# Seven products in place of eight for one more pair of k-tiles, and 1-f from a second sigmoid, in a bidirectional recurrence layer

## The chip, the cores and the metric

The kernel runs on one core of a Trainium2 chip. The metric is the time of one execution on the device in microseconds, the median of several runs.

## What is computed

One encoder layer over 256 tokens of width 2048, in fp32. Cut to what matters here:

```python
hn = _rmsnorm(h, norm_w[i])
proj = hn @ w_in[i]                                  # 2048 x 18432
q, v, f_fwd, f_bwd, z_a, b_gate, c_gate, h_b, z_b = jnp.split(proj, IN_SPLITS, axis=-1)
# each direction, 16 heads of 128, chunks of 64 tokens, q = silu(q):
f = lb + (1.0 - lb) * jax.nn.sigmoid(f_logit)
log_f = jnp.log(f)
k = 1.0 - f
b = jnp.cumsum(log_f, axis=-2)
q_rel = q * jnp.exp(b - b_mid)
k_rel = k * jnp.exp(b_mid - b)
scores = jnp.einsum('bhntk,bhnsk->bhnts', q_rel, k_rel)   # masked, times v; plus the carried state
# then: o_a normed per head, * silu(z_a); the short convolution's branch; w_out; gate; final norm
```

The weights of one layer are read once, some 260 MB with what the kernel writes and reads again.

## The kernel before

TensorE does the fp32 products as three products of rounded halves: each fp32 number is split into a high part (ScalarE, the cast of L121) and a low part, the rest (VectorE, the subtraction of L122), for the weights as they stream in as for the activations. Weights come by DMA on SP's queue into three raw buffers of 1 MB (`Stream.load`, L100), and `Stream.get` opens the parts three ahead of use, into five buffers of split parts (`spl`). `three` (L545 to L549) is one product of 128 rows, 128 tokens and 512 columns: three matmuls.

The projections of q, the two forget gates, v and z_a run for eight groups of two heads, called pairs 0 to 7 here, taken two at a time (`two_pairs`, i = 0, 2, 4, 6). For each of two pairs TensorE does the forward gate, the backward gate and q (`gemm_in`, L425 and L427, then `evac`, L487 on ScalarE and L488 on VectorE); then v and z_a of both pairs together (`gemm_vz`). v and z_a are summed over sixteen k-tiles of 128, in eight pairs of k-tiles q = 0 to 7 (`VZ_ORDER`, in the code called q as well). A pair of k-tiles is a 2 by 2 product of blocks (two halves of tokens, two k-tiles, and the two column blocks v and z_a). In plain form that is eight products of `three`, 24 matmuls. For the q in `VZ_SUMS` it is done with seven (`half`, the part behind `which.index(q)`), 21 matmuls, by sums of blocks of weights and of activations in Strassen's manner. Four banks of PSUM collect what goes into both outputs and are added at the end (L469 to L477).

The sums of activations, for each q of `VZ_SUMS`, are made once, in the projection stage of pair 2, and kept (`xsum`). The sums of weights are made in one of two ways. For the q in `VZ_OWN`, VectorE makes them in the raw buffer (`add_up`, L83, three additions of 128x1024). For other q in `VZ_SUMS`, DMAs make them in DRAM: `prepare` copies four blocks from the weights into a buffer in DRAM (SP's queue), `add_up` in the kernel's body adds to them in three steps of accumulating DMAs issued by GpSimd (L338, L342), and the stream then loads three blocks and the 1 MB of sums. Before the change all q of `VZ_SUMS` are in `VZ_OWN`, so no such sum is made for v and z_a; the output projection, later, makes sixteen (`sums`).

For each pair, `mix_forgets` (L605 to L629) scales by the norms on GpSimd (L492), takes the sigmoid of both gates' logits (L614, ScalarE), then for each direction and head the logarithm (L623, ScalarE) into `lf`, and 1-f on VectorE from the sigmoid, with `noml` = -(1-lb) and `oml` = 1-lb (L627). `mix_pair` (L667 on) makes the running sums (L678, L684), the differences to the middle of each chunk (L691, L694: `dd`), the factors across chunks (`ge`, from three small sums L700 to L702 and an exponential L703), and per direction exp(dd) into `pf` (L705), exp(-dd) into `dd` (L706), 1-f times `dd` (L707) and q times `pf` (L708). GpSimd makes from them `kc` and `qc` (L716, two of each, one for each direction) and `kx` (L722). `products` then does small matmuls of 128x32 on TensorE, sixteen kinds for each head and half (L735); their first reads `qc` of direction 1 and `dd`. Behind them are `cx` (L779, `kx` times `qc`), a masked copy on VectorE (L783) and a sum on GpSimd (L784: `s`).

What sets the order: TensorE's program is in the order of the code. A clock of ticks, one to three for a k-tile or pair of k-tiles of a projection, calls what `at(dt, fn)` has set. So the products of the first of two pairs stand early in the v/z_a stage, and those of the second pair (pair 3, 5, 7) run 32 ticks behind the end of it, in the first projection stage of what comes next (behind pair 7 that is the first projection of the convolution, whose `cg` is scaled on GpSimd at L492). On ScalarE, VectorE and GpSimd a scheduler sets the order of the instructions from priorities (`high_priority`: the splits and the evacuations stand ahead) and from when it reckons their inputs to be ready.

## Time and profile before

| | |
|---|---|
| median of 3 runs | 1111.57 us (1110.87 to 1111.96) |
| profiled execution, its time | 1112.2 us |
| profiled execution, its span | 1110.5 us |
| granted clock of TensorE | 0.998 |
| first product of pairs 3, 5, 7 (from the span's start) | 262.94, 380.37, 497.80 us |

The span is the time from the first to the last instruction that the profiler recorded. PE is TensorE and PEld its loading of weights, DVE is VectorE, ACT ScalarE, POOL GpSimd, SP the engine whose queue issues the loads. A row of the timeline gives the start, the duration, the engine, the line, the operation, and in square brackets how long the engine was idle ahead of it and what it waited for. Matmuls overlap: the distance of two starts is what one costs, not the duration in the row. A row of a group gives the busy time of all its instructions, the mean of one in ns, and the idle time ahead of them. [...]

### The profile page before, as it was taken

The page shows a single profiled execution, that of the slowest core. Times are in us where ns is not written, and L with a number is a line of the kernel's source. Part 1 is how long each engine was busy: PE and PEld are TensorE (multiplying, and loading weights), DVE is VectorE, ACT ScalarE, POOL GpSimd, SP SyncE. Part 2 cuts the span into 40 slices and gives each one's busy share as a digit, 9 for nine tenths or more (in the row PEclk, how much of TensorE's full clock was granted, in tenths as well). Part 3 has the DMA queues.
Part 4 walks back from the last instruction along what each step waited for, and adds up shares of the span by engine and source line. Part 5 has one row for each costly group of instructions (what it writes and reads, how often), then busy time and mean ns, then how long its engine had stood idle before and what let it go on. Part 6 is the DMA issues. An engine that isn't in the chain of part 4 may idle for free.

```text
span 1110.5 us, 16882 instructions
## 1 busy us (share of the span) xinstructions
PE 1100.5 (99%) x6455; PEld 945.7 (85%) x6455; DVE 851.4 (77%) x1127; ACT 677.3 (61%) x946; POOL 269.1 (24%) x215
## 2 busy tenths in 40 slices
PE   9999999999999999999999999999999999999997
PEld 8888888888888888888888888888888888888886
DVE  7799578896889778997657758856667888887673
ACT  6786577667876697575545535535546575575562
POOL 1045015203530325043334223424331000000101
PEclk9999999999999999999999999999999999999999
DMA  9755454564457744758999998999979887887542
GB/s 340 272 187 190 153 190 157 171 242 153 161 162 258 292 152 152 231 172 228 298 310 250 270 334 231 282 345 254 288 196 306 318 299 286 286 312 253 193 133 76
DMA packets 69808, 260.44 MB, mean 235 GB/s; under 512 B 7008, under 2 KB 16608, under 8 KB 52192
## 3 DMA queue, kind: packets, MB, share of 16 engines
q1 hardware_dynamic: 60480, 242.25, 62.1%
q0 software_dynamic: 8960, 16.78, 10.0%
q8 instruction: 51, 0.84, 0.3%
q10 hardware_dynamic: 288, 0.34, 0.1%
q14 instruction: 29, 0.24, 0.1%
HBM read 257.25 MB, written 35.65 MB: 264 GB/s over the span
## 4 chain that ended last, share of the span: by engine, by line
PE 98%; DMA 1%; ACT 0%; SPq 0%; DVE 0%; DVEq 0%; issue 0%; ACTq 0%
PE a L427 37%; PE a L425 19%; PE avz L547 3%; PE avz L548 3%; PE avz L549 3%; PE pg L1027 3%; PE pg L1026 3%; PE pg L1028 3%; PE pa L547 2%; PE pa L548 2%; PE pa L549 2%; PE a L446 1%; PE a L448 1%; PE a L447 1%; PE pb_sc L548 1%; PE pb_sc L549 1%
## 5 line engine op out<-in xcount | busy, mean ns | idle before, releaser
L122 DVE TENSOR_TENSOR spl<-raw,spl 128x1024 fp32r<-128x1024 f32 (+2 forms) x419 | 505.0, 1219 | 163.6 <-ACT spl L121 160.2
L427 PE MATMUL a<-xs,spl 128*128 128x512 f32 x1792 | 617.3, 395 | 0.6 <-ACT spl L121 0.6
L121 ACT CAST spl<-raw 128x1024 fp32r<-128x1024 f32 (+2 forms) x419 | 414.1, 999 | 255.0 <-PE a L425 81.9
L425 PE MATMUL a<-xs,spl 128*128 128x256 f32 x1792 | 483.8, 278 | 0.0
L427 PEld LDWEIGHTS a<-xs,spl 128*128 128x128 f32 x1792 | 332.2, 188 | 73.6 <-ACT spl L121 1.0
L425 PEld LDWEIGHTS a<-xs,spl 128*128 128x128 f32 x1792 | 334.6, 188 | 5.8 <-DVE spl L122 0.5
L1143 POOL TENSOR_TENSOR hh<-hh,fw 128x512 f32<-128x512 f32 (+1 forms) x9 | 11.0, 1227 | 250.7 <-ACT gt L1142 248.0
L487 ACT COPY r<-a 128x256 f32<-128x256 f32 x112 | 40.5, 368 | 37.3 <-PE a L425 35.8
L547 PE MATMUL avz<-spl,xs 128*128 128x512 f32 x138 | 54.0, 391 | 0.0
L549 PE MATMUL avz<-spl,xs 128*128 128x512 f32 x138 | 53.7, 389 | 0.0
L548 PE MATMUL avz<-spl,xs 128*128 128x512 f32 x138 | 53.7, 389 | 0.0
L1026 PE MATMUL pg<-spl,ht 128*128 128x512 f32 (+1 forms) x120 | 45.2, 377 | 0.0
L1027 PE MATMUL pg<-spl,ht 128*128 128x512 f32 (+1 forms) x120 | 45.1, 376 | 0.0
L1028 PE MATMUL pg<-spl,ht 128*128 128x512 f32 (+1 forms) x120 | 45.0, 375 | 0.0
L716 POOL TENSOR_TENSOR qc<-pf,ge 128x256 f32<-128x256 f32 x16 | 18.3, 1148 | 105.8 <-ACT dd L706 91.8
L492 POOL TENSOR_TENSOR xf<-xf,rbc 128x1024 f32<-128x1024 f32 x8 | 19.9, 2486 | 94.0 <-DVE rbc L403 50.2
L121 ACT CAST spl<-early 128x1024 fp32r<-128x1024 f32 (+1 forms) x29 | 28.7, 990 | 19.1 <-PE pb_y L549 7.5
L122 DVE TENSOR_TENSOR spl<-early,spl 128x1024 fp32r<-128x1024 f32 (+1 forms) x29 | 32.9, 1147 | 9.2 <-ACT spl L121 8.8
L547 PE MATMUL pa<-spl,mixa 128*128 128x512 f32 x88 | 34.5, 392 | 0.0
L549 PE MATMUL pa<-spl,mixa 128*128 128x512 f32 x88 | 34.3, 389 | 0.0
L548 PE MATMUL pa<-spl,mixa 128*128 128x512 f32 x88 | 34.2, 389 | 0.0
L716 POOL TENSOR_TENSOR kc<-dd,ge 128x256 f32<-128x256 f32 x16 | 27.7, 1728 | 19.8 <-DVE dd L707 13.6
(321 smaller groups left out, 1641.7 us busy)
## 6 DMA issues: line engine op xcount, KB each, us to landing
raw<-in_w_in_dram SPq DMA_DIRECT2D x106, 1024.0 KB, 6.9
raw<-in_w_in_dram SPq DMA_DIRECT2D x100, 256.0 KB, 3.9
raw<-in_w_out_dram SPq DMA_DIRECT2D x36, 512.0 KB, 5.2
sums<-in_w_out_dram SPq DMA_DIRECT2D x32, 512.0 KB, 10.6
raw<-in_w_in_dram SPq DMA_DIRECT2D x26, 512.0 KB, 5.2
raw<-sums SPq DMA_DIRECT2D x13, 1024.0 KB, 5.3
raw<-in_w_gate_dram SPq DMA_DIRECT2D x9, 1024.0 KB, 5.1
sums<-in_w_out_dram POOLq DMA_DIRECT2D x16, 512.0 KB, 10.1
```

The costliest lines, as they stand in the source:

```text
L121: self.nc.scalar.copy(out=v[:, :, 0], in_=r)
L122: self.nc.vector.tensor_tensor(out=v[:, :, 1], in0=r, in1=v[:, :, 0], op=ALU.subtract)
L425: pe.matmul(a[:, :T], lhsT=lhsT, rhs=xs[:, kt, 0, :], start=False, stop=(kt == NKT - 1))
L427: pe.matmul(a, lhsT=lhsT, rhs=xs[:, kt, :, :].rearrange("p s n -> p (s n)"), start=(kt == 0), stop=False)
L487: act.copy(out=r, in_=acc[m][:, 1, :])
L547: pe.matmul(acc, lhsT=ah, rhs=w[:, 0], start=start, stop=False)
L548: pe.matmul(acc, lhsT=ah, rhs=w[:, 1], start=False, stop=False)
L549: pe.matmul(acc, lhsT=al, rhs=w[:, 0], start=False, stop=stop)
L716: pool.tensor_tensor(out=c64(dst[:, d]), in0=c64(src[:, d, :, half * P : (half + 1) * P]), in1=g.unsqueeze(3).broadcast_to([P, 2, 2, CH]), ...
L1026: pe.matmul(acc[m], lhsT=lh, rhs=wh, start=(kt == 0), stop=False)
L1027: pe.matmul(acc[m], lhsT=lh, rhs=wl, start=False, stop=False)
L1028: pe.matmul(acc[m], lhsT=ll, rhs=wh, start=False, stop=(kt == nk - 1))
```

## The change

It has two parts that the diff shows, and the order that comes of them.

The first part puts q = 5 into `VZ_SUMS` but not into `VZ_OWN`. In each of the three v/z_a stages that use `half` (i = 2, 4, 6) that pair of k-tiles is done with seven products, and its sums of weights are made in DRAM by `prepare` and `add_up`, called at ticks 50, and 166, 196 and 220 (98, 104 and 110 for the first two pairs). `xsum` has four sets in place of three.

The second part makes 1-f as (1-lb) times the sigmoid of the negated logit. The first sigmoid goes to `lf`, and the logarithm is taken there in place; a second sigmoid with scale -1 takes the place of the logits in `xf`. The 32 instructions of L627 and `noml` go. Where L707 multiplied `xf` and `dd` for both heads in one instruction, `scalar_tensor_tensor` now does it for each head, with `oml` as its scalar (L705 in the kernel after). To make room for the larger `xsum`, some constants move to other buffers.

```diff
-    VZ_ORDER, VZ_SUMS, VZ_OWN = range(8), (2, 4, 6), (2, 4, 6)
+    VZ_ORDER, VZ_SUMS, VZ_OWN = range(8), (2, 4, 5, 6), (2, 4, 6)
...
-    wz = const.tile([P, P], F32, name="wz")
+    early = const.tile([P, 2048], F32, name="early")
+    wz = early[:, 1024 : 1024 + P]
...
-    mx = const.tile([P, 2, 16], F32, name="mx")
-    et = const.tile([P, 2, 2, 16], F32, name="et")
-    esum = const.tile([P, 2, 16], F32, name="esum")
+    mx = xp.tile([P, 2, 16], F32, name="mx")
+    et = xp.tile([P, 2, 2, 16], F32, name="et")
+    esum = xp.tile([P, 2, 16], F32, name="esum")
...
-    noml = const.tile([P, 2, 16], F32, name="noml")
...
-        dve.tensor_scalar(noml, oml, -1.0, None, op0=ALU.mult)
...
-    rw = [const.tile([P, P], F32, name=f"rw{m}") for m in range(2)]
...
+        rw.append(ap_.tile([P, 2, P], F32, tag="s", name="rw"))
...
-        act.activation(xf, xf, AF.Sigmoid)
+        lf = ap_.tile([P, 2, 2, T], F32, tag="lf", name=f"lf{i}")
+        act.activation(lf, xf, AF.Sigmoid)
         sg = ap_.tile([P, 2, T], F32, tag="sg", name=f"sq{i}")
         act.activation(sg, qt, AF.Sigmoid)
+        act.activation(xf, xf, AF.Sigmoid, scale=-1.0)
         pool.tensor_tensor(out=qt, in0=qt, in1=sg, op=ALU.mult)
 
-        lf = ap_.tile([P, 2, 2, T], F32, tag="lf", name=f"lf{i}")
         for d in range(2):
             for h in range(2):
                 hd = 2 * i + h
                 act.activation(
-                    lf[:, d, h, :], xf[:, d, h, :], AF.Ln,
+                    lf[:, d, h, :], lf[:, d, h, :], AF.Ln,
                     bias=lb[:, d, hd : hd + 1], scale=oml[:, d, hd : hd + 1],
                 )
-                dve.tensor_scalar(
-                    xf[:, d, h, :], xf[:, d, h, :], noml[:, d, hd : hd + 1], oml[:, d, hd : hd + 1],
-                    op0=ALU.mult, op1=ALU.add,
-                )
...
             act.activation(pv[d], dv[d], AF.Exp)
             act.activation(dv[d], dv[d], AF.Exp, scale=-1.0)
-            dve.tensor_tensor(out=dv[d], in0=xf[:, d], in1=dv[d], op=ALU.mult)
+            for h in range(2):
+                dve.scalar_tensor_tensor(
+                    out=dv[d][:, h], in0=xf[:, d, h], scalar=oml[:, d, 2 * i + h : 2 * i + h + 1], in1=dv[d][:, h],
+                    op0=ALU.mult, op1=ALU.mult,
+                )
             dve.tensor_tensor(out=pv[d], in0=qt, in1=pv[d], op=ALU.mult)
```

With fewer instructions on VectorE and more on ScalarE, the scheduler sets a different order on three engines. TensorE keeps its own, apart from the products of q = 5. The place shown is the first projection stage behind the v/z_a stage of pairs 2 and 3, in which pair 3's `mix_pair` runs. Here is GpSimd there, before (L716 makes `qc` and `kc`, L722 `kx`, L784 `s`):

```order
48 L784 TENSOR_TENSOR s_2059<-early 128x256 x2
49 L716 TENSOR_TENSOR qc_2400<-pf_2376,ge_2386 128x256
50 L716 TENSOR_TENSOR kc_2399<-dd_2377,ge_2386 128x256
51 L716 TENSOR_TENSOR qc_2400<-pf_2376,ge_2386 128x256
52 L716 TENSOR_TENSOR kc_2399<-dd_2377,ge_2386 128x256
53 L722 TENSOR_TENSOR kx_2405<-kc_2399,ge_2386 128x512
54 L784 TENSOR_TENSOR s_2617<-early 128x256
```

and after (the lines are one further on; `vz_5` is the buffer in DRAM for the sums of q = 5):

```order
48 L785 TENSOR_TENSOR s_2071<-early 128x256 x2
49 L717 TENSOR_TENSOR qc_2419<-pf_2393,ge_2403 128x256
50 L717 TENSOR_TENSOR kc_2418<-dd_2394,ge_2403 128x256 x2
51 L723 TENSOR_TENSOR kx_2424<-kc_2418,ge_2403 128x512
52 L717 TENSOR_TENSOR qc_2419<-pf_2393,ge_2403 128x256
53 L336 DMA vz_5_82<-in_w_in_dram 256x1x256 x2
54 L785 TENSOR_TENSOR s_2638<-early 128x256
```

The second `qc`, that of direction 1, has moved from between the two `kc` to behind `kx`, and the issue of the accumulating DMAs follows it.

ScalarE at the same place, before (L121 is the cast of a split, L487 half of an evacuation, L703 makes `ge`, L705 and L706 the exponentials, L802 the squares of an output):

```order
221 L703 ACTIVATE ge_2386<-gx 128x20
222 L706 ACTIVATE dd_2377<-dd_2377 128x512
223 L705 ACTIVATE pf_2376<-dd_2377 128x512
224 L802 ACTIVATE jk_2457,ss_1332<-o_2448 128x128
225 L487 COPY r<-a_4_0_2355 128x256
226 L121 CAST spl_2513<-raw_2511 128x4x256
227 L487 COPY r<-a_4_1_2356 128x256
228 L706 ACTIVATE dd_2377<-dd_2377 128x512
229 L802 ACTIVATE jk_2457,ss_1332<-o_2448 128x128 x3
230 L121 CAST spl_2532<-raw_2511 128x4x256
```

and after (`ge` is L700 there, the exponentials L702 and L703):

```order
224 L702 ACTIVATE pf_2393<-dd_2394 128x512
225 L121 CAST spl_2534<-raw_2532 128x4x256
226 L487 COPY r<-a_4_0_2372 128x256
227 L487 COPY r<-a_4_1_2373 128x256
228 L121 CAST spl_2553<-raw_2532 128x4x256
229 L700 ACTIVATE ge_2403<-gx 128x20
230 L703 ACTIVATE dd_2394<-dd_2394 128x512
231 L702 ACTIVATE pf_2393<-dd_2394 128x512
232 L703 ACTIVATE dd_2394<-dd_2394 128x512
233 L121 CAST spl_2574<-raw_2572 128x4x256
234 L121 CAST spl_2653<-raw_2572 128x4x256
```

`ge` and two exponentials have moved from ahead of the cast of the first of these parts, and one from between the two casts, to behind the second cast.

VectorE after the change, in the same stretch (L122 is the subtraction of a split, L488 the other half of an evacuation, L705 the new product, L709 the product with q, L784 the masked copy that waits for the products):

```order
255 L709 TENSOR_TENSOR pf_2393<-qt_1684,pf_2393 128x512
256 L122 TENSOR_TENSOR spl_2534<-raw_2532,spl_2534 128x4x256
257 L488 TENSOR_TENSOR xf_2370<-a_4_0_2372,r 128x256
258 L122 TENSOR_TENSOR spl_2553<-raw_2532,spl_2553 128x4x256
259 L488 TENSOR_TENSOR xf_2370<-a_4_1_2373,r 128x256
260 L705 SCALAR_TENSOR_TENSOR dd_2394<-xf_1683,oml,dd_2394 128x256 x3
261 L122 TENSOR_TENSOR spl_2574<-raw_2572,spl_2574 128x4x256
262 L705 SCALAR_TENSOR_TENSOR dd_2394<-xf_1683,oml,dd_2394 128x256
263 L709 TENSOR_TENSOR pf_2393<-qt_1684,pf_2393 128x512
264 L122 TENSOR_TENSOR spl_2653<-raw_2572,spl_2653 128x4x256
265 L488 TENSOR_TENSOR xf_2370<-a_4_0_2511,r 128x256
```

Three of the four products of 1-f stand behind the split of the second part (`spl_2553`), the fourth and the product with q behind that of the third.

More of the change, by code (lines that the diff above doesn't have):

```diff
@@ L273, in tile_hymba_encoder @@
     pool.memset(ones, 1.0)
-    early = const.tile([P, 2048], F32, name="early")
     smask = early[:, 0:T]
@@ L395, in x_norms @@
         dve.reciprocal(out=rx, in_=rx)
+        rw.append(ap_.tile([P, 2, P], F32, tag="s", name="rw"))
         for m in range(2):
-            dve.tensor_copy(rw[m], rx[:, m : m + 1].broadcast_to([P, P]))
+            dve.tensor_copy(rw[0][:, m], rx[:, m : m + 1].broadcast_to([P, P]))
+    rw = []
     def norms_spread():
@@ L401, in norms_spread @@
         for m in range(2):
-            pe.matmul(rps[:, m * P : (m + 1) * P], lhsT=rw[m], rhs=ident, start=True, stop=True)
+            pe.matmul(rps[:, m * P : (m + 1) * P], lhsT=rw[0][:, m], rhs=ident, start=True, stop=True)
         dve.tensor_copy(rbc, rps[:, :T])
```

## Prediction

> **What bounds the kernel now.** I read the page first: the span, the busy shares, and the chain that ended last.
>
> ```profile
> span 1110.5 us, 16882 instructions
> PE 1100.5 (99%) x6455; PEld 945.7 (85%) x6455; DVE 851.4 (77%) x1127; ACT 677.3 (61%) x946; POOL 269.1 (24%) x215
> PE 98%; DMA 1%; ACT 0%; SPq 0%; DVE 0%; DVEq 0%; issue 0%; ACTq 0%
> ```
>
> TensorE is busy for 1100.5 of 1110.5 us and makes 98% of the chain; every other engine has slack on average. So only two things can move the end: how many matmuls TensorE has, and whether it now waits where it did not. The sum is made against the profiled execution: 1112.2 us, the span of 1110.5 and 1.7 outside it, which is 0.6 above the median of 1111.57. The differences are then carried to the median. A difference under 0.2%, 2.2 us, can't be told from none by a measurement of this kernel.
>
> **The matmuls saved.** The timeline of TensorE in the v/z_a stage of pairs 4 and 5 shows one 512-column product after another:
>
> ```profile
> 329.71 0.39 PE L547 MATMUL scps<-spl,xsum 128*128 128x512 f32 x1
> ...
> 333.79 0.39 PE L547 MATMUL avz<-spl,xs 128*128 128x512 f32 x1
> ```
>
> 18 starts lie between these rows: 4.08 us, 0.227 us each (the 0.39 of a row overlaps its neighbours). A pair of k-tiles as seven products takes 7×3 = 21 such matmuls where the plain form takes 24. One more pair in each of three stages saves 9 matmuls: 9×0.227 = **2.04 us**, 0.18%. The list of matmuls is otherwise the same, in the same order. [...]
>
> **The new form of 1-f, by work.** The groups by line:
>
> ```profile
> L627 DVE TENSOR_SCALAR xf<-xf,noml,oml 128x256 f32<-128x256 f32 x32 | 14.8, 472 | 4.6 <-ACT lf L623 4.6
> L707 DVE TENSOR_TENSOR dd<-xf,dd 128x512 f32<-128x512 f32 x16 | 13.6, 851 | 0.6 <-ACT dd L706 0.6
> L938 DVE SCALAR_TENSOR_TENSOR cg<-ub,vec,cg 128x256 f32<-128x256 f32 x32 | 14.5, 477 | 0.2
> L614 ACT ACTIVATE xf<-xf 128x1024 f32<-128x1024 f32 x8 | 8.5, 1062 | 6.9 <-POOL xf L492 6.9
> ```
>
> VectorE loses the 32 of L627 (14.8 us) and the 16 of L707 (13.6), and gets 32 products with a scalar of half that width, for which L938 is the nearest row: 32×0.477 = 15.3. It gains about 13 us, ScalarE gets 8×1.06 = 8.5 more. Neither bounds the kernel, so by itself this is worth nothing. What counts is where the instructions stand.
>
> **Where they stand: the product groups of pairs 3, 5 and 7.** The groups for the scores of the second pair of each two run on TensorE in the first stage behind v/z_a; their first matmul reads qc. These are the starts of three such groups:
>
> ```profile
> 262.94 0.30 PE L735 MATMUL scps<-qc,dd 128*32 128x128 f32 x2
> 380.37 0.30 PE L735 MATMUL scps<-qc,dd 128*32 128x128 f32 x2
> 497.80 0.30 PE L735 MATMUL scps<-qc,dd 128*32 128x128 f32 x2
> ```
>
> TensorE does not wait ahead of them now: these rows show no idle time before them. VectorE ahead of 262.94:
>
> ```profile
> 254.82 0.41 DVE L488 TENSOR_TENSOR xf<-a,r 128x256 f32<-128x256 f32 x1
> ...
> 261.35 1.23 DVE L122 TENSOR_TENSOR spl<-raw,spl 128x1024 fp32r<-128x1024 f32 x1 [1.54 <-ACT spl L121]
> 263.10 0.43 DVE L488 TENSOR_TENSOR xf<-a,r 128x256 f32<-128x256 f32 x1 [0.52 <-ACT r L487]
> ```
>
> ScalarE in the same stretch:
>
> ```profile
> 250.82 0.22 ACT L703 ACTIVATE ge<-gx 128x20 f32<-128x20 f32 x1 [0.47 <-DVE gx L702]
> 251.47 0.61 ACT L705 ACTIVATE pf<-dd 128x512 f32<-128x512 f32 x1
> ...
> 257.50 1.05 ACT L121 CAST spl<-raw 128x1024 fp32r<-128x1024 f32 x1 [1.15 <-PE a L425]
> 260.27 1.05 ACT L121 CAST spl<-raw 128x1024 fp32r<-128x1024 f32 x1 [1.72 <-PE a L425]
> ```
>
> GpSimd there, and at a later group, 45 us on:
>
> ```profile
> 251.56 0.62 POOL L716 TENSOR_TENSOR qc<-pf,ge 128x256 f32<-128x256 f32 x1 [45.92 <-ACT dd L706]
> 256.70 1.91 POOL L722 TENSOR_TENSOR kx<-kc,ge 128x512 f32<-128x512 f32 x1
> 298.28 5.01 POOL L716 TENSOR_TENSOR kc<-dd,ge 128x256 f32<-128x256 f32 x1 [3.66 <-DVE dd L707]
> 305.51 1.05 POOL L722 TENSOR_TENSOR kx<-kc,ge 128x512 f32<-128x512 f32 x1
> ```
>
> GpSimd now ends kx, its last, at 258.61, 4.3 us ahead of the products. In the order after the change two things differ. On ScalarE ge and three of the four exponentials stand behind two casts that they stood ahead of or between. On GpSimd the second qc, which the first product reads, comes last of all, behind both kc and kx. The walk, on the clock of before:
>
> ScalarE: its last two casts start 2.77 us apart, released by TensorE; the one ahead of them then can't start before 257.50−2.77 = 254.73, and ends at 255.78. Behind it ge (0.22) and three exponentials (0.61) end at 256.0, 256.6, 257.2 and 257.8; the next cast runs to 258.9, the one after stays at 260.27 to 261.3. VectorE: the split behind the first of these casts to 257.05, L488 (0.41) to 257.5, two of the new products to 258.4, a third to 258.9, the next split to 260.2, the fourth product to 260.7, the product with q (0.69, the row of L708 below) to 261.4, the last split from there to 262.6, then nothing before 263.1.
>
> GpSimd: kc, kc, kx, qc are 0.62+0.62+1.05+0.62 = 2.9 us alone, and the first kc has its input at 258.4. If nothing holds it, the second kc starts at 260.7, kx ends at 262.4, qc at 263.0: a wait of 0.1 us. But VectorE holds it. The kc at 298.28 took 5.01 us where 0.62 is the time of one this size alone (qc's row); VectorE meanwhile:
>
> ```profile
> 298.12 1.22 DVE L122 TENSOR_TENSOR spl<-raw,spl 128x1024 fp32r<-128x1024 f32 x1
> 299.26 0.68 DVE L708 TENSOR_TENSOR pf<-qt,pf 128x512 f32<-128x512 f32 x1
> ...
> 301.60 1.22 DVE L122 TENSOR_TENSOR spl<-raw,spl 128x1024 fp32r<-128x1024 f32 x1
> 302.73 0.42 DVE L488 TENSOR_TENSOR xf<-a,r 128x256 f32<-128x256 f32 x1
> ```
>
> GpSimd stayed out while VectorE ran one such instruction after another, and its 0.6 us fit behind 302.73, where L488 reads PSUM. So in the walk it gets in where VectorE pauses: at 261.4 if it wins there (qc ends at 264.3), or at 262.6 (265.5). Between these, 264.9: **2.0 us** of waiting for the group of pair 3, bounds 0.1 and 2.6. Pair 5's has the same order: 2.0 again. [...]
>
> Pair 7's group has more ahead of it on GpSimd, from the next part of the kernel:
>
> ```profile
> 492.31 1.75 POOL L492 TENSOR_TENSOR cg<-cg,early 128x512 f32<-128x512 f32 x1
> 494.00 1.21 POOL L338 DMA_DIRECT2D sums<-in_w_out_dram  x1
> 494.76 1.10 POOL L716 TENSOR_TENSOR kc<-dd,ge 128x256 f32<-128x256 f32 x1
> ```
>
> In before, cg and the issue of a DMA stand between the second qc and the second kc; after the change both stand ahead of either kc. If they get in before VectorE closes up, they cost nothing more (2.0). If not, cg (1.05, as kx) and the issue (0.76, from 494.00 to the next row) come on top: 3.8, at most 2.6+1.8 = 4.4. I take 3.2, nearer to the second, since cg's input comes from the L488 just ahead of the new products. All waits: 2.0+2.0+3.2 = **7.2 us**, bounds 0.3 and 9.6.
>
> **The v/z_a streak.** Blocks 4, 5 and 6 are now all of seven products. This is VectorE now, over one cycle of a seven-product and a plain block and into the next:
>
> ```profile
> 209.53 4.34 DVE L122 TENSOR_TENSOR spl<-raw,spl 128x1024 fp32r<-128x1024 f32 x4 [0.19 <-ACT spl L121]
> ...
> 219.73 4.34 DVE L122 TENSOR_TENSOR spl<-raw,spl 128x1024 fp32r<-128x1024 f32 x4 [0.85 <-ACT spl L121]
> ...
> 226.57 2.50 DVE L122 TENSOR_TENSOR spl<-raw,spl 128x1024 fp32r<-128x1024 f32 x2
> ```
>
> and on TensorE the first use of the second of the last two splits:
>
> ```profile
> 232.00 0.39 PE L547 MATMUL avz<-spl,xs 128*128 128x512 f32 x1
> ```
>
> A cycle is 10.20 us with 0.85 idle. Block 5 needs 3.5 splits of 1.22 where it needed 2: VectorE 9.35+1.83 = 11.2, TensorE 10.20−0.68 = 9.5. VectorE falls 1.7 behind; the two splits from 226.57 end at 229.07, 2.9 ahead of their use at 232.00. 1.2 remains, and two more parts with a hand-over between the engines each (up to 0.85, the idle time above) can eat it. I take 0; the bound is 1.7+1.7−2.9 = 0.5, say 0.7 us a stage, 2.1 in all.
>
> **The rest, at nothing.** The added sums are four SP DMAs and four GpSimd DMAs a stage, and the plain load of 1 MB becomes three blocks and 1 MB on SP's queue:
>
> ```profile
> raw<-in_w_in_dram SPq DMA_DIRECT2D x106, 1024.0 KB, 6.9
> ```
>
> The GpSimd ones stand behind the late qc in the order. Their cover is the stretch of two pairs' projections in which they are issued; without it one load comes late, by up to the 6.9 us of this row. The moved constants are filled and read ahead of or beside matmuls as before.
>
> **Rivals.** (A) The forecast: all three groups wait, −2.04+7.2 = +5.2, 1112.2 to 1117.4 in the profiled execution, 1116.7 on the median; with sums of waits from 4.3 to 9.6, 1113.8 to 1119.1. Chance 0.60. (B) GpSimd slips in between VectorE's instructions, as kc did in 1.00 us in the row below, and qc is there at 263.0: waits of 0.3, 1109.8, so not slower, and the change does just its nine matmuls. It decides if kc enters by 258.9 and kx by 261.4 without holding up the rest. For it: short holds exist in before. Against: VectorE's walk has no pause before 261.4. Chance 0.13.
>
> ```profile
> 252.65 0.68 DVE L708 TENSOR_TENSOR pf<-qt,pf 128x512 f32<-128x512 f32 x1
> 252.81 1.00 POOL L716 TENSOR_TENSOR kc<-dd,ge 128x256 f32<-128x256 f32 x1 [0.63 <-DVE dd L707]
> ```
>
> (C) Partial: waits between 0.3 and 4.3, which the saving nearly pays, 1109.8 to 1113.8, say 1112. The turn to slower is 2.04+2.2 = 4.3 us of waits. Chance 0.20. (D) The streak starves as well: 7.2+2.1, 1118.8. Chance 0.07.
>
> **How the numbers follow.** Slower is A and D, 0.67; B lies 0.16% under before, so a third of it may come out as faster, 0.05; the rest, 0.28, is within the bound. The range leaves out most of B below and the ends of D above: 1110.2 to 1119.5.
>
> **What would show it.** The first qc product of pairs 3, 5 and 7 starts 2 to 3 us later against the projection matmul ahead of it, released by GpSimd's qc, and kc's or kx's rows are long. No pause of TensorE in the v/z_a stages; nine matmuls fewer. Wrong if those products start at once, or if blocks 6 and 7 wait for VectorE's splits.

## The result, and the profile after

The kernel after takes 1130.07 us (median of 6 runs, 1126.31 to 1133.34) against 1111.65 for the kernel before on the same chip (6 runs, 1110.87 to 1112.02): ratio 1.0165, interval 1.014 to 1.019, so **slower by 1.65%**. The forecast was 1116.7, with an upper end of 1119.5. The sign was right, the size was not: 18.4 us were lost where 5.1 were expected. The profiled execution took 1132.3 us, span 1130.5, 20.0 above the span of before. Of the six, three took 1126.3 to 1127.9 us at a granted clock of 0.997, as in before, and three, the profiled one among them, 1132.3 to 1133.3 at 0.993 to 0.995.

The page of the kernel after, its span, busy times and chain:

```profile
span 1130.5 us, 16939 instructions
PE 1108.8 (98%) x6446; PEld 947.0 (84%) x6446; DVE 851.7 (75%) x1122; ACT 685.0 (61%) x957; POOL 272.1 (24%) x227
PE 75%; DVE 8%; ACT 7%; DMA 4%; POOL 2%; issue 2%; SPq 1%; DVEq 0%; ACTq 0%; POOLq 0%
```

There are nine matmuls fewer (6446), as forecast, and yet TensorE is busy 8.3 us longer; VectorE did not gain its 13 us (851.7 against 851.4). The chain is no longer TensorE alone: a quarter of it runs over the engines that TensorE waits for. These are TensorE's waits in the kernel after (line, for whom; us in total, times, the longest). `scps` are the products, `ogt` the transposes of the gated outputs `ogz`, `ex`, `ey` and `avz` the banks that v and z_a are summed in, `wps` matmuls at the start:

```profile
PE scps L736 <- POOL qc L717: 8.4, 3, 4.0
PE ogt L655 <- DVE ogz L645: 1.6, 4, 0.7
PE ey L548 <- DVE spl L122: 1.4, 3, 0.8
PE wps L267 <- DVE early L262: 1.1, 1, 1.1
```

The first three make 11.4 us (`wps`, at the start, is in before too). The rest is in matmuls that take longer and in what a wait costs beyond its idle time: of the matmul released at 231.59 below, 0.81 us is idle, and it starts 1.20 after the one ahead of it, where 0.227 is usual. Matching the starts of the same matmul in the two traces gives where the 20.0 us arise:

| place | us later |
|---|---|
| product groups of pairs 3, 5, 7, each with what runs right behind it | 1.3 + 4.8 + 5.3 = 11.4 |
| v/z_a stages, net of 0.68 saved in each | 1.1, -0.1, 0.1 (3.2 lost in all, 1.4 of it in the waits for `ey`) |
| transposes of the gated outputs (`ogt`), first pairs 2 and 4 | 1.4 + 1.2 = 2.6 |
| output projection (840 to 1003 us), with a wait of 0.4 for a split | 4.5 |
| the start, and pieces under 0.2 | 0.4 |

**The product groups.** The same three rows as in the prediction, in the kernel after:

```profile
265.38 0.30 PE L736 MATMUL scps<-qc,dd 128*32 128x128 f32 x2 [1.23 <-POOL qc L717]
387.37 0.30 PE L736 MATMUL scps<-qc,dd 128*32 128x128 f32 x2 [3.21 <-POOL qc L717]
511.93 0.42 PE L736 MATMUL scps<-qc,dd 128*32 128x128 f32 x2 [3.95 <-POOL qc L717]
```

and GpSimd and VectorE ahead of the first:

```profile
259.47 0.73 POOL L717 TENSOR_TENSOR kc<-dd,ge 128x256 f32<-128x256 f32 x1 [0.82 <-DVE dd L705]
261.82 0.94 POOL L717 TENSOR_TENSOR kc<-dd,ge 128x256 f32<-128x256 f32 x1 [1.62 <-DVE dd L705]
262.84 1.91 POOL L723 TENSOR_TENSOR kx<-kc,ge 128x512 f32<-128x512 f32 x1
264.71 0.61 POOL L717 TENSOR_TENSOR qc<-pf,ge 128x256 f32<-128x256 f32 x1
```

```profile
258.42 1.30 DVE L705 SCALAR_TENSOR_TENSOR dd<-xf,oml,dd 128x256 f32<-128x256 f32 x3
259.72 1.56 DVE L122 TENSOR_TENSOR spl<-raw,spl 128x1024 fp32r<-128x1024 f32 x1
261.21 0.47 DVE L705 SCALAR_TENSOR_TENSOR dd<-xf,oml,dd 128x256 f32<-128x256 f32 x1
```

`qc` is last and TensorE waits for it: the wait is the forecast one. But neither `kc` is long (0.73 and 0.94 where 5.01 was feared): GpSimd had nothing to do until the fourth product of 1-f, which stands behind a split. `kx` takes 1.91 where other groups show 1.05, at each of the three groups, and did so there in before (256.70 in the prediction's rows). At pair 7 the first `kc` is long, 2.15 where 0.62 is its time alone:

```profile
505.79 2.15 POOL L717 TENSOR_TENSOR kc<-dd,ge 128x256 f32<-128x256 f32 x1
```

Ahead of pair 5's group ScalarE's cast waits for a load, and the exponentials stand behind the cast:

```profile
376.37 1.05 ACT L121 CAST spl<-raw 128x1024 fp32r<-128x1024 f32 x1 [2.46 <-DMA raw<-in_w_in_dram]
```

**The clock.** TensorE's time and granted clock in consecutive windows of 3.41 us around the groups of pairs 3, 5 and 7, in the kernel after (columns: us, busy, clock, DMA share, GB/s):

```profile
262.25:265.66 3.41, 2.18 (x30) 1.00 1.06 307
265.66:269.07 3.41, 3.41 (x94) 1.00 0.99 332
...
385.13:388.54 3.41, 1.17 (x80) 1.00 0.74 235
388.54:391.95 3.41, 3.41 (x28) 0.50 1.01 275
391.95:395.36 3.41, 3.41 (x21) 1.00 0.55 86
...
508.01:511.42 3.41, 0.00 (x0) 1.00 0.97 149
511.42:514.84 3.42, 2.91 (x83) 0.50 0.88 287
```

But for the end of this execution the clock is at 0.50 in two stretches only, 388.54 to 391.95 and 511.42 to 514.84: 3.41 us each, and the 119.47 us between them are 35 times 3.41; the windows above stand on that grid. With 1.23 us idle in one (pair 3) the next is at full clock; with 2.24 idle (pair 5) the next runs at 0.50 throughout, and with all of one idle (pair 7) as well. The delay at pair 5 is 4.8 us for a wait of 3.2; the 1.6 above it is the work of the window at 0.50: a matmul of 512 columns in it has the next one start 0.43 us on (391.18 to 391.61), behind it 0.23, so its 3.41 us brought an estimated half of the work. Pair 7's delay is 5.3 for 4.0, with one such window too. So 8.4 of the 11.4 us are waits, and some 3 are half clock, in the execution profiled.

**The v/z_a stage.** TensorE's first wait there, and SP's issue of the loads ahead of it, in the kernel after:

```profile
231.59 0.50 PE L548 MATMUL ey<-spl,xsum 128*128 128x512 f32 x1 [0.81 <-DVE spl L122]
```

```profile
213.27 0.33 SPq L96 DMA_DIRECT2D raw<-vz  x1
219.75 1.92 SPq L96 DMA_DIRECT2D raw<-in_w_in_dram  x4
```

The second row is the load of block 6 (a block is here a pair of k-tiles), and `ey` at 231.59 is block 6's. In before the load is issued at 212.16 (`212.16 1.92 SPq L96`), here at 219.75: it needs a raw buffer, and the next comes free with the last split of block 4, at 219.73. Block 6 waiting for VectorE's splits is one of the signs by which the prediction was to be wrong.

### The profile page after: what moved, and what is told of

It is laid out like the page before. It is cut to its first block, busy times and chain, and to the rows that moved or that the text cites. A ratio compares the mean times of both kernels' runs of the same rounds, so it can differ in the third digit from the quotient of the medians.

```text
span 1130.5 us, 16939 instructions
## 1 busy us (share of the span) xinstructions
PE 1108.8 (98%) x6446; PEld 947.0 (84%) x6446; DVE 851.7 (75%) x1122; ACT 685.0 (61%) x957; POOL 272.1 (24%) x227
## 4 chain that ended last, share of the span: by engine, by line
PE 75%; DVE 8%; ACT 7%; DMA 4%; POOL 2%; issue 2%; SPq 1%; DVEq 0%; ACTq 0%; POOLq 0%
PE a L427 28%; PE a L425 14%; DVE spl L122 4%; ACT spl L121 3%; DMA raw<-in_w_in_dram 3%; PE pg L1029 3%; PE pg L1027 3%; PE pg L1028 3%; PE pa L548 1%; PE pa L549 1%; PE avz L547 1%; PE pa L547 1%; PE avz L549 1%; PE avz L548 1%; PE a L446 1%
## 5 line engine op out<-in xcount | busy, mean ns | idle before, releaser
L122 DVE TENSOR_TENSOR spl<-raw,spl 128x1024 fp32r<-128x1024 f32 (+2 forms) x425 | 502.8, 1198 | 181.7 <-ACT spl L121 179.2
L121 ACT CAST spl<-raw 128x1024 fp32r<-128x1024 f32 (+2 forms) x425 | 418.1, 996 | 254.2 <-PE a L425 79.0
L487 ACT COPY r<-a 128x256 f32<-128x256 f32 x112 | 40.1, 369 | 39.6 <-PE a L425 36.8
L547 PE MATMUL avz<-spl,xs 128*128 128x512 f32 x120 | 47.1, 393 | 0.3 <-DVE qt L488 0.3
L549 PE MATMUL avz<-spl,xs 128*128 128x512 f32 x120 | 46.8, 390 | 0.0
L548 PE MATMUL avz<-spl,xs 128*128 128x512 f32 x120 | 46.8, 390 | 0.0
L122 DVE TENSOR_TENSOR spl<-early,spl 128x1024 fp32r<-128x1024 f32 (+1 forms) x29 | 32.9, 1147 | 10.7 <-ACT spl L121 10.7
L121 ACT CAST spl<-early 128x1024 fp32r<-128x1024 f32 (+1 forms) x29 | 28.7, 991 | 19.2 <-PE pb_y L549 7.8
L944 POOL TENSOR_TENSOR cg<-cg,hb 128x512 f32<-128x512 f32 x8 | 13.7, 1714 | 82.3 <-DVE hb L488 82.3
```

Of the source, the lines that this page charges most:

```text
L121: self.nc.scalar.copy(out=v[:, :, 0], in_=r)
L122: self.nc.vector.tensor_tensor(out=v[:, :, 1], in0=r, in1=v[:, :, 0], op=ALU.subtract)
L487: act.copy(out=r, in_=acc[m][:, 1, :])
L547: pe.matmul(acc, lhsT=ah, rhs=w[:, 0], start=start, stop=False)
L548: pe.matmul(acc, lhsT=ah, rhs=w[:, 1], start=False, stop=False)
L549: pe.matmul(acc, lhsT=al, rhs=w[:, 0], start=False, stop=stop)
```

## The experiments

All times are beside runs of the kernel before on the same chip (median 1111.6 to 1113.1); the ratio has its 95% interval behind it. Two experiments that ran on different chips compare by their ratios; their medians can differ by 1.4 us for that reason alone.

The theories at the outset: the **queue** theory of the prediction (`qc` is late since it stands last on GpSimd); its rival, that the **exponentials** behind the casts set it; for v/z_a, **VectorE** overdrawn by three blocks in a row; for the output projection, the order of something against the **place** of the buffers in SBUF.

### The two parts apart

**Second part alone** (`VZ_SUMS` as before, the new 1-f, `noml`'s 128 bytes per partition gone).

> The part on 1-f alone, VZ_SUMS as before; buffers start 128 bytes lower, as in the run before. On GpSimd both qc stand ahead of kx here, as in before. Theory of the queue order (the products of pairs 3, 5, 7 wait since the second qc stands last): no wait there, 1111.6, or 1116 if the place of the buffers slows the output projection. Rival (the later exponentials and products with 1-f make the wait by themselves): waits of 1 to 4 us at each of the three groups, 1116 to 1122.

1118.28 us, 1.0059 (1.0044 to 1.0074), 2 us above the 1116. No wait ahead of any product group, and no half clock: 0.998 over the execution, as in before. The transposes come 0.56 and 0.54 later, 3.9 us arise in the output projection, and 1.2 in a stretch of the convolution's projections (683 to 742 us). The change touches the code of neither.

**First part alone** (q = 5 with seven products, old 1-f, `noml` kept).

> The part on q = 5 alone, 1-f as before, the constants moved as in the change, noml kept; buffers start 2048 bytes lower. On GpSimd the second qc of pairs 3, 5 and 7 stands last here too. Theory of the queue order: the waits of 8.8 us ahead of the three groups are here, and the v/z_a stages wait as in the changed kernel: 1120 to 1126. Rival (1-f makes the waits): none ahead of the products, 1111.6 - 2.0 + 2 to 3 of the v/z_a stages = 1112 to 1113. By the place of the buffers the output projection is at 0.227 us here.

1128.98, 1.0163 (1.0141 to 1.0185), above what either theory gave. The profiled execution took 1133.85, the other three 1128.3 to 1129.3, so its trace shows more lost than the median has. TensorE's waits in it:

```profile
PE scps L737 <- POOL qc L718: 7.2, 3, 3.3
PE ey L550 <- DVE spl L122: 2.8, 3, 0.9
PE ey L549 <- ACT spl L121: 2.0, 3, 0.8
```

So the late `qc` comes with the seven products and not with the new 1-f. ScalarE's order is that of the kernel after: in pair 3's stage three exponentials start from 258.97 on, behind a cast at 257.90, where in the second part alone they stand ahead of the casts. That a larger backlog of casts and splits made the scheduler do this is a reading and was not tried. And in this execution the v/z_a stages lose 3.1 us each net of what they save. Around the end of that of pairs 4 and 5 the windows of TensorE read:

```profile
352.28:355.69 3.41, 1.87 (x8) 1.00 0.46 193
355.69:359.11 3.42, 3.42 (x10) 0.50 0.58 177
```

1.54 us idle in one window, in pieces under 1 us, and the next runs at half clock. In the stage of pairs 2 and 3 it was 1.60 us (0.67 and 0.93, ahead of 232.13), and the matmuls behind start 0.43 us apart (233.44 to 233.87), where 0.227 is usual. The granted clock of the whole execution, 0.992 against 0.998 in before, is worth some four such windows by an estimate (0.006 of 1132 us, 1.7 us in each). The two parts do not add: the change with both loses less in v/z_a and more at the products. Why was not tried.

### The output projection: place

**The kernel before with 128 bytes less of constants.**

```diff
-    noml = const.tile([P, 2, 16], F32, name="noml")
+    noml = vec[:, 6:8, :]
```

> The kernel before with noml laid into a part of vec that is dead by then: every buffer behind the constants (raw, spl, xs) starts 128 bytes lower, and nothing else changes. In the changed kernel these buffers start 2176 bytes lower (128 more than a multiple of 2048) and the matmuls of the output projection came every 0.232 us where before had 0.227, some 4.4 us in all. If the place of the buffers does that, this kernel is 4.4 us slower (1116) and its output projection shows 0.232 us. If it comes from the pauses and the clock, or from the execution, this kernel takes 1111.6 and shows 0.227.

1116.4, 1.004 (1.0025 to 1.0055), from the same instructions. 21 starts of TensorE in the output projection, first and last, in the kernel before:

```profile
899.69 0.39 PE L548 MATMUL pb_y<-spl,mixb 128*128 128x512 f32 x1
...
904.45 0.39 PE L548 MATMUL pb_sc<-spl,mixb 128*128 128x512 f32 x1
```

and in this experiment:

```profile
899.62 0.40 PE L548 MATMUL pb_sc<-spl,mixb 128*128 128x512 f32 x1
...
904.53 0.39 PE L548 MATMUL pb_y<-spl,mixb 128*128 128x512 f32 x1
```

4.76 us against 4.91: 0.227 us a matmul against 0.234. In the kernel after it is 4.88, 0.232. The other stages of this experiment keep the pace that they have in before, within 0.5 us up to there.

**The kernel after with the 128 bytes back**, as an unused tile:

```diff
+    const.tile([P, 2, 16], F32, name="pad")
```

> The changed kernel with an unused 128 bytes among the constants, so that raw, spl and xs start a multiple of 2048 bytes below where before has them. If the slower matmuls of the output projection hang on the place alone: back to 0.227 us there and 4.5 us less, 1125.5. If they also hang on the pauses ahead of them, no change: 1130. The other waits stay.

1127.45, 1.0136 (1.012 to 1.0152). The output projection runs at 0.227 again. The span of the profiled execution falls by 5.5, from 1130.5 to 1125.0, of which 3.4 are in that stage; the medians fall by 2.6 only (3.2 by the ratios), where 4.5 were expected; the runs of the kernel after spread over 7. The same tile added to the second part alone:

> The 1-f part alone, as run before, with 128 unused bytes in noml's stead, so that all buffers lie as in before. The place was worth 4.8 us; by that alone 1118.3 - 4.8 = 1113.5, with waits of about 1 us ahead of two groups of transposes. If its waits are more than that, or vary with the place: 1116 or more.

1112.79, 1.0008 (0.9999 to 1.0017), where it was 1118.28 without: some 5.5 us are place, the 1.2 of the convolution's projections among them. The new 1-f itself costs about 1 us, the two transposes (1.15 later in the trace); the interval does not quite exclude none.

**Which place.** In the kernel before, an unused tile of 128 bytes ahead of the buffers of split parts:

```diff
+    padp = ctx.enter_context(tc.tile_pool(name="padp", bufs=1))
+    padp.tile([P, 32], F32, name="pad")
```

> The kernel before with 128 unused bytes between the raw buffers and the split ones: raw stays, spl and xs lie 128 bytes higher. If the place of the split buffers, which the output projection's matmuls read, makes the 0.232 us: it is there, 1116. If the raw buffers' or the constants' place does: 0.227, 1111.6.

1115.94, 1.004 (1.0026 to 1.0055), 0.232 a matmul. And all moved down by 256 bytes (`noml` into `vec`, `mx` into another pool):

> The kernel before with noml laid into vec and mx into another pool: raw, spl and xs lie 256 bytes lower. If any move from the place in before slows the output projection: 0.232 us and 1116. If it hangs on the place modulo 256: 0.227 and 1111.6.

1112.26, 1.0002 (0.9992 to 1.0012), 0.227. So it is the address of the buffers from the split parts on, and no order of instructions: a matmul takes 0.232 us with them 128 bytes up, 0.234 with 128 down and 0.232 with 2176 down (the kernel after), and 0.227 with 256 and with 2048 down (the kernel after with the 128 bytes back). Why the output projection feels it, and other stages not or in one kernel only, is open.

### The products: queue or exponentials

**Queue.** In the kernel after, `kc`, `qc` and `kx` are kept in the order of the code, so `qc` comes ahead of `kx`:

```diff
-            pool.tensor_tensor(
+            place(pool.tensor_tensor(
...
-        pool.tensor_tensor(out=kx, in0=kc, ...)
+        place(pool.tensor_tensor(out=kx, in0=kc, ...))
```

> The changed kernel with kc, qc, kc, qc, kx of the second pairs kept in that order on GpSimd; the order on ScalarE and VectorE stays. Theory (the second qc is late because it stands behind kx, 1.91 us in the profile): 1.3, 1.9 and 1.9 us less at the three groups, and no or one halving of the clock in place of two: 1122 to 1124. Rival (the exponentials and the products with 1-f, behind the casts, set the start by themselves): 1129 or more.

1128.83, 1.0153 (1.0137 to 1.0168): a miss. The products still wait 0.6, 2.0 and 3.5 us, where it was 1.2, 3.2 and 4.0 without the edit: the place on the queue is 2.4 of the 8.4. In front of `kx` or behind it, `qc` has to wait for the second `kc` and the last product with q on VectorE, and in front of it its own row takes 1.5 to 1.6 us, where 0.62 is its time alone.

**Exponentials.** In the kernel after, the exponentials and what VectorE makes of them stand ahead of the splits in these stages:

```diff
+        with tc.high_priority(offset=400 if here else 0):
             act.activation(ge, gx, AF.Exp)
             for d in range(2):
...
```

> The changed kernel with ge, the exponentials and the products of 1-f and q of the second pairs given priority over the splits, so that on ScalarE they stand ahead of the casts and on GpSimd both qc ahead of kx. Theory: the 8.8 us of waits ahead of the products and the two halvings of the clock behind them (2.6) go: 1130.1 - 11.4 = 1118.7. Rival: the splits come late in their place, and it stays at 1126 or more. If the slower output projection (4.4 us) hangs on the pauses, it goes as well: 1114.

1120.1, 1.0073 (1.0056 to 1.009): as expected. TensorE's waits there, without any for `qc`:

```profile
PE ogt L655 <- DVE ogz L645: 1.8, 4, 0.7
PE wps L267 <- DVE early L262: 1.1, 1, 1.1
PE ey L548 <- DVE spl L122: 1.1, 3, 0.4
```

and no window at half clock before the end (0.998 over the execution). Ten of the 18.4 us lost hang on where a few exponentials of 0.6 us, and VectorE's products of them, stand among the casts and splits. The edit moves both, and `qc` comes ahead of `kx` with them; which of the moves does how much was not separated.

### The v/z_a stages: VectorE, or a buffer

**Another block.** The kernel with the 128 bytes back, with block 1 in place of 5, so that no three blocks of seven products follow one another:

```diff
-    VZ_ORDER, VZ_SUMS, VZ_OWN = range(8), (2, 4, 5, 6), (2, 4, 6)
+    VZ_ORDER, VZ_SUMS, VZ_OWN = range(8), (1, 2, 4, 6), (2, 4, 6)
```

> The run with the place put right, with q = 1 in place of q = 5 as the fourth block of seven products: 2, 4 and 6 keep their own sums, and a plain block lies between them again. Theory (three blocks of seven products in a row overdraw VectorE, and the backlog of splits is what pushes the exponentials and qc back): no wait in the v/z_a stages behind the first block, none or little ahead of the products, the 2.0 us saved: 1109.6 to 1112, the upper end if the transposes still wait. Rival (the sums in DRAM with their loads are the cost, wherever the block lies): waits as before, 1120 or more.

1117.78, 1.0054 (1.0039 to 1.0069). No product group waits, and the second and third stage gain 0.37 and 0.39. But the first stage loses 3.5: `ex` of block 2 comes to wait 2.3 us for a copy of ScalarE (`sx`), and the matmuls behind it start 0.42 us apart (204.65 to 205.07), at half clock. Block 1 with the old 1-f and priority for that copy and for the gate of z_a:

> 1-f as before, four blocks of seven products at q = 1, 2, 4, 6 (2, 4, 6 with their own sums), the buffers at the good place, and priority for the copy of cx and for the gate of z_a. Theory (what the changed kernel lost was the place, the backlog of three blocks in a row, and the order that came of it): no wait ahead of the products or the transposes, only a short one for the bank of cx in the first v/z_a stage: 1109.6 to 1111, under before. Rival (the sums in DRAM, or the fourth set of banks' use so early, cost as much as the 2.0 us saved): 1111.6 or more.

1115.12, 1.0029 (1.0018 to 1.004), short of what was expected: `ey` waits for a split in each stage, 2.5 us in all. In this kernel the waits for splits follow the block to its new place.

**VectorE relieved.** First part alone, with the sums of blocks 4 and 6 made in DRAM too (`VZ_OWN` = (2,)), which takes six additions off VectorE a stage:

> As the run with the part on q = 5 alone (1-f as before, buffers at the good place, q = 2, 4, 5, 6 with seven products), but only q = 2 has its sums made by VectorE; those of 4, 5 and 6 come from DRAM. VectorE then has 4.3 us of splits for each of these blocks against 4.8 us of TensorE, where with sums of its own it has 6.9. Theory (VectorE's sums in blocks 4 and 6, with no plain block between, starve TensorE): the waits in the v/z_a stages and the halvings of the clock there go, 1116 to 1121 with what is left ahead of the products. Rival (loads from DRAM late, or the traffic): 1127 or more, since there are three times as many of them.

1137.72, 1.0223 (1.0197 to 1.0248). The stages lose 2.7, 5.9 and 5.1. With less work for VectorE it is worse, which speaks against the theory of the overdrawn VectorE. It does not settle it, since blocks 4 and 6 now need more loads and buffers too; the experiment on the buffer does, which leaves VectorE's work as it is. With the exponentials and the gate put first as well:

> The run before with the exponentials of the second pairs ahead of the splits, which took the waits ahead of the products away in an earlier run, and priority for the gate of z_a. Theory: nothing is left of the changed kernel's waits, 1109.6 to 1111. Rival (DRAM sums cost by themselves): 1113 or more.

1134.37, 1.0192 (1.017 to 1.0214): the product waits are gone, those in v/z_a stay. One of its windows bears on the clock:

```profile
234.77:238.18 3.41, 1.82 (x7) 1.00 0.66 267
238.18:241.60 3.42, 3.42 (x17) 1.00 0.79 263
```

1.59 us idle, and the next window is at full clock, where 1.54 in the first part alone went ahead of half clock. So in these runs the idle time of a window does not decide by itself.

**A buffer of its own.** A block with sums in DRAM loads three blocks and the sums, 1.75 MB, and so holds two of the three raw buffers; a block whose sums VectorE makes in place holds one. In the first part alone, the three plain blocks of q = 5 now go to a place of their own (that of `pf` and `dd`, unused then):

```diff
+            if j in self.placed:
+                self.raws[j] = self.placed[j]
...
+        ws.placed[ws.where[blocks[B_V, i][5][0]][0]] = ap_.tile([P, 2048], F32, tag="pd", name=f"q5raw{i}")
...
-        pf = ap_.tile([P, 2, 2, T], F32, tag="pf", name=f"pf{i}")
-        dd = ap_.tile([P, 2, 2, T], F32, tag="dd", name=f"dd{i}")
+        pd = ap_.tile([P, 2, 2, 2, T], F32, tag="pd", name=f"pd{i}")
+        pf, dd = pd[:, 0], pd[:, 1]
```

> As the run with the part on q = 5 alone, but the three plain blocks of q = 5 are loaded into a tile of their own (the place of pf and dd, free in that stretch), not into one of the three raw buffers. A block with its sums in DRAM takes two of the three raw buffers, so the load of block 6 now waits for the last split of block 4, where before it waited for that of block 3. Theory (that wait makes the late load, and the late load the waits in the v/z_a stages): they go for the most part, with the halvings of the clock there, 1129.0 - 8 to 10 = 1119 to 1121, the waits ahead of the products left. Rival (VectorE has too much work in blocks 4 to 6): no change, 1127 or more.

1125.27, 1.0109 (1.0094 to 1.0125), 3.7 us less than without the edit on the medians and 6 by the ratios, where 8 to 10 were expected. The load of block 6 on SP's queue is back where it was:

```profile
210.90 0.33 SPq L97 DMA_DIRECT2D raw<-vz  x1
213.17 1.92 SPq L97 DMA_DIRECT2D raw<-in_w_in_dram  x4
```

and the three stages now gain 0.61, 0.61 and 0.59, nearly the whole 0.68 each, where the profiled execution without the edit lost 3.1 each. So the waits in v/z_a came from the buffer, as the theory says; that they were worth less over all runs than in that execution fits its being the longest of four. What is left is the product groups: 8.9 us of waits for `qc` and, behind pairs 5 and 7, half clock (0.993 over the profiled execution), more than was reckoned for them. Why the products wait longer here (8.9) than without the edit (7.2) was not settled.

### Both mends, and what the change is worth then

That kernel with the exponentials first as well:

> The run before with the exponentials of the second pairs ahead of the splits. By the theory nothing of the changed kernel's waits is left: 1109.6 to 1111.5. If VectorE's work in blocks 4 to 6 still starves TensorE by 0.5 us a stage or more, or the priority delays the splits: 1112 to 1116.

1111.58, 0.9991 (0.9981 to 1.0001), the span of its profiled execution 1109.3. Its waits:

```profile
PE wps L270 <- DVE early L265: 1.1, 1, 1.1
PE ogt L664 <- DVE ogz L654: 0.8, 2, 0.6
PE pa L554 <- DVE spl L125: 0.2, 1, 0.2
```

Of the 2.04 us that nine matmuls are worth 1.8 are there (0.60, 0.61, 0.61); the first transposes take 1.2 back. These moved from tick 32 to 36:

```diff
-                    at(32, lambda e=e: turn(i + e, ogs[e], "yx"[e]))
+                    at(32 if i else 36, lambda e=e: turn(i + e, ogs[e], "yx"[e]))
```

> The run before (seven products for q = 5, its plain blocks in a place of their own, exponentials first, 1-f as before) with the first transposes four ticks later, where they waited 1.1 us. If that wait was the last: 1110.4 or so, 0.1% under before. If the later transposes run into the next use of their bank: 1111.6 or more.

1111.49, 0.9989 (0.9981 to 0.9998), the best version, a tenth of a per cent under the kernel before, and short of the 1110.4. Their wait is gone, and two others have grown (`pa` 0.5, `avz` 0.3). With the new 1-f added and the 128 bytes kept:

> The run before with the new form of 1-f as well, and 128 unused bytes for noml: the whole change, with the place and the waits mended. If the 1-f part costs only the order of the gate of z_a on GpSimd (0.4 to 1.4 us at each of two groups of transposes): 1111.5 to 1113. If it costs nothing now: as the run before it.

1113.29, 1.0009 (1.0 to 1.0018), its transposes 1.6 and 1.3 later: the second part gives back what the first had gained. Its only wait on TensorE besides the start:

```profile
PE ogt L660 <- DVE ogz L650: 1.9, 4, 0.9
```

One attempt made things worse by itself: block 1, both parts, the exponentials first, and all transposes moved from tick 32 to 48.

> As the run before, with the exponentials of the second pairs ahead of the splits as well, and the transposes of the outputs 16 ticks later. If all waits that the changed kernel shows are named rightly: 1109.6, 2.0 under before. If the priority or the later transposes bring waits of their own: 1111 to 1114.

1128.75, 1.0162 (1.0142 to 1.0182):

```profile
PE cx L782 <- POOL qt L620: 6.4, 2, 3.2
PE cx L782 <- DVE mixa L660: 4.3, 1, 4.3
```

With the transposes sixteen ticks later `cx` waits for what comes of them (`mixa`) and for a product of GpSimd. The run moves the exponentials as well, so which edit brings the second wait is open.

## Why the prediction was right in sign and wrong in size

Of the 14.8 us between the forecast of +5.2 and the +20.0 of the profiled execution, four things make nearly all: half clock behind the waits that were forecast, a late load in v/z_a, the place of the buffers, and the transposes. The forecast had put the second and third at nothing and had no term for the others.

**The matmuls saved: right.** Nine fewer, and 1.8 of 2.04 us seen once nothing hides them.

**1-f worth nothing by work: right for the end, wrong for VectorE.** The new product was priced by L938 (477 ns). In the kernel after:

```profile
L705 DVE SCALAR_TENSOR_TENSOR dd<-xf,oml,dd 128x256 f32<-128x256 f32 x32 | 20.9, 695 | 2.1 <-ACT dd L703 2.0
```

32 times 0.695 would be 22.2, not 15.3 (the busy time, 20.9, counts overlaps once). Ten of the 32 ran with no GpSimd instruction beside them, in 474 ns on average, none over 477; the other 22 took 796 on average, up to 1524. So the price was right for the instruction alone, and what it left out is that most of them are longer beside GpSimd's products. The 1-f part is not free: about 1 us alone, 1.8 on top of the best version (1113.29 against 1111.49).

**The product groups: right place, right releaser, near in size, in part by luck.** 8.4 of waits against 7.2, within its bounds of 0.3 and 9.6; by group 1.2, 3.2 and 4.0 against 2.0, 2.0 and 3.2. The walk's order held; each `qc` came last. Half right was the reason given for its lateness: pair 7's first `kc` is long (2.15), but no row shows a hold as the 5.01 was (that VectorE held GpSimd there was the author's reading of rows that ran side by side, and not shown otherwise), and the position on GpSimd's queue is 2.4 of the 8.4. The walk also took `kx` at 1.05, the row of another group; at these groups it is 1.91, before as after. With 1.91 the walk has `qc` at 263.9 without any hold, a wait of 0.9 at pair 3, where 1.2 was measured. It is the exponentials behind the casts, with VectorE's products behind them, which the walk had as a step on the way, whose return to the front removes all of it. At pair 5 the cast ahead of them also waited 2.46 us for a load, which the walk did not have. Missing was the price of a wait for what comes behind it: half clock, some 3 us in the profiled execution.

**The v/z_a streak at 0: the step that failed first.** 3.2 us lost in the change, and 3.8 a stage (3.1 net and the 0.68 saved) in the profiled execution of the first part alone. The working looked at VectorE's sum of work, where the limit was a raw buffer. The right sentence stood under "The rest, at nothing": a load that comes late. It was covered there with the stretch in which the sums are made, though the load that came late was block 6's, held by how many buffers a block takes.

**The moved constants at nothing: wrong by some 4 us.** The output projection is 3.9 to 4.8 us longer in the four kernels compared. They were judged by when they are filled and read; what counted was where all buffers behind them came to lie: 2176 bytes lower, at 0.232 us a matmul, where 2048 lower gave 0.227.

**Not looked at: the transposes.** 2.6 us. `ogz` needs z_a's gate `zt`, a product on GpSimd that in the kernel after stands behind `kx` and the issue of a DMA:

```profile
296.51 1.92 POOL L723 TENSOR_TENSOR kx<-kc,ge 128x512 f32<-128x512 f32 x1
298.37 0.83 POOL L340 DMA_DIRECT2D vz<-vz  x1
298.94 1.58 POOL L635 TENSOR_TENSOR zt<-zt,sz 128x512 f32<-128x512 f32 x1
```

`zt` starts at 298.94, in before at 292.94. That the order on GpSimd is what delays them was read from these rows and not tried by itself.

The sum by the measured sizes: 11.4 for the products with their half clock, 3.2 for v/z_a, 4.5 for the place, 2.6 for the transposes and 0.4 for the rest make 22.1; less 2.04 that is 20.1, the 20.0 of the spans but for rounding. Of these the forecast had only the first, without the half clock.

## What to carry to other kernels

A saving of 0.2% on the bounding engine (2.04 us here) is smaller than one wait in each stage (8.4 us at the three product groups), so cost each resource that a step holds (buffers, queue places, addresses), not only its work. Where TensorE waits, ask what its clock does in the window behind (0.50 at two of the three groups here). And when something moves in SBUF, time the kernel with an unused tile in its place first, before looking for causes in the order.

## What the runs showed of the hardware

- TensorE's granted clock was 0.50 for two stretches of 3.41 us in the middle of the kernel after, 35 times 3.41 us apart; of the 3.41 us ahead of each, 2.24 and 3.41 were idle. How long TensorE is idle did not decide by itself: 1.54 and 1.60 us (first part alone) went ahead of half clock, 1.23 (kernel after) and 1.59 (sums in DRAM, exponentials first) did not. What else decides is open. At the products a stretch at half clock cost some 1.3 to 1.6 us, and executions of one kernel differ in the clock: 1126.3 us at 0.997, 1133.3 at 0.993 (kernel after).
- The 512-column matmuls of the output projection, 0.227 us each in before, took 0.232 with the buffers of split parts 128 bytes higher, 0.234 with them 128 lower and 0.232 with 2176 lower (the kernel after), and 0.227 with 256 and with 2048 lower. By the medians 128 bytes higher cost 4.0 us and 128 lower 4.8.
- `scalar_tensor_tensor` of 128x256 took 477 ns on average in one place (L938, before) and 695 in another (L705, kernel after). At L705 none of the ten without a GpSimd instruction beside it took over 477 ns; every longer one, up to 1524, ran beside a product of GpSimd. At L938 none ran beside a product of GpSimd, only beside issues of DMAs, and none took over 487. That the product beside it is the cause is read from this and was not tried.
